# Prompt attention in plain fp32, two heads at a time, in place of products of high and low parts

## The chip, the cores and the metric

One core of one Trainium2 chip runs the whole program in one launch. The metric is the time of one execution in device microseconds (us); lower is better. The core's engines are called PE (matrix products), PEld (the loading of the stationary operand into PE), DVE (vector), ACT (scalar functions and copies), POOL (the second vector engine) and SP (which issues most DMAs). PE's array has 128 rows, over which a product sums, and 128 columns, its output partitions.

## The reference

One layer of a hybrid decoder for a prompt of 1024 tokens and for 8 x 8 sampled tokens. The input projection is split among an RWKV-7 recurrence, a short convolution and stick-breaking attention; then come an output projection, a squared-ReLU MLP and a gated per-layer embedding. What matters here is the attention of the prompt, 8 heads of 64 dimensions over 1024 positions:

```python
z = jnp.einsum('bqhd,bkhd->bhqk', q_blk.astype(jnp.float32), kf) * scale + bias_f
mask = k_pos[None, :] < q_pos[:, None]
log_beta = jnp.where(mask, jax.nn.log_sigmoid(z), -jnp.inf)
log_keep = jnp.where(mask, jax.nn.log_sigmoid(-z), 0.0)
later = lax.cumsum(log_keep, axis=3, reverse=True) - log_keep
wts = jnp.exp(log_beta + later)
return jnp.einsum('bhqk,bkhd->bqhd', wts, vf)
```

with `q` and `k` normalised per head beforehand (`rmsnorm`). In the recurrence, the keys are normalised per head too (`kk * lax.rsqrt(jnp.sum(kk * kk) + 1e-12)`).

## The kernel before

Large products run on PE in a reduced fp32 format (F32R, "fp32r" in the profile), which PE multiplies faster and less exactly than plain fp32 (F32). To keep fp32's accuracy an operand is split into a high part (a copy rounded to F32R, on ACT) and a low part (the remainder, by a subtraction on DVE or POOL), and a product is the sum of products of the parts. Small products, of the recurrence above all (lines 541 to 671, and 740 to 785 for the sampled tokens), are in plain fp32 and use halves or quarters of the array: an operand on partitions 0 to 63 or 64 to 127 sits in one row half, an output on such partitions in one column half.

The prompt's attention takes four steps.
- `project` (L847) writes the rows of q, k, v of 128 tokens. For v it makes a tile `spl` with a head's 64 high columns next to its 64 low ones and stores it in the DRAM scratch `v_s`. `stack` (L870) transposes q and k and stores high and low parts in the scratch `stk_s`, so that a head has 128 rows: 64 high, 64 low.
- `prep` (L932) loads, for one head, `stk_k`, `stk_q`, the swapped `stk_x` (low over high) and `vs`.
- `weights` (L952) makes, for one head and a block of 256 queries (two tiles of 128), the scores in chunks of up to 512 keys: L961 multiplies keys with `stk_q`, L962 adds the product with `stk_x`, so that all four products of parts are in. ACT takes two sigmoids of each chunk (L963, L964), POOL masks the diagonal (L968), DVE scans (L970) and multiplies (L972; on POOL for every other tile in the second call). The result is `beta`.
- `values` (L975) transposes `beta` (L990), splits it into `wth` and `wtl` (`split`, L59: ACT copies, DVE subtracts, L60 and L61), and multiplies both with `vs` (L1000, L1001), which gives the sums with v's high and low columns in the two halves of the output's partitions; L1003 and L1004 add them.

`attention` runs twice: for queries 0 to 511 it is interleaved by `run` with the convolution (`CA` says how many steps of each), for queries 512 to 1023 it follows the output projection of the first 512 tokens. `AA` and `AB_` say how many units `weights` runs ahead of `values`. Scores have two PSUM banks (`zbank`), transposed weights two (`wbank`), outputs one (`obank`).

The order in which the instructions stand on each engine is set when the program is built: a scheduler with a model of the times goes through what is ready, so attention's instructions end up woven into those of the convolution (L173 to L175), the output projection and the MLP's first products (L1144 to L1146), and not in the order in which they are written. Each engine then runs its row in that order.

Of the kernel before, what the change touches and what calls it, by code (L numbers as in the profile page):

```python
# [42 lines left out]
AA = 2  # L43
CA = (5, 4)
AB_ = 2
# [3 lines left out]
def hybrid_step(ctx: ExitStack, tc: tile.TileContext, I, O):  # L49
# [6 lines left out]
    def f(t):  # L56
        return t.bitcast(F32)

    def split(dst_hi, dst_lo, src):  # L59
        S.copy(dst_hi, src)  # L60
        V.tensor_sub(dst_lo, src, f(dst_hi))  # L61
# [29 lines left out]
    stk_s = dram.tile([2, 8, 2, 64, NP], F32, name="stk_s")  # L91
    v_s = dram.tile([8, 8, 128, 128], F32, name="v_s")
# [29 lines left out]
    ident_r = consts.tile([128, 128], F32R)  # L122
    G.tensor_copy(ident_r, ident)
# [276 lines left out]
    for j in range(2):  # L400
# [13 lines left out]
        rbs = []  # L414
        for a in range(2):
            rb = pe_tile("rb", F32R)
            rbs.append((rb, rp.tile([128, 2, 64], F32R, name=f"rb8{a}")))
            for d, i0, i1 in ((rb[:, :1024], 0, 8), (rbs[a][1].rearrange("p s d -> p (s d)"), 8, 9)):
                d = d.rearrange("p (i s d) -> p i s d", i=i1 - i0, s=2)
                src = rk[:, i0:i1, :, None].to_broadcast([128, i1 - i0, 2, 64])  # L420
                if a == 0:
                    V.tensor_copy(d, src)
                else:
                    h = rbs[0][0][:, :1024] if i0 == 0 else rbs[0][1].rearrange("p s d -> p (s d)")
                    V.tensor_sub(d, src, f(h).rearrange("p (i s d) -> p i s d", i=i1 - i0, s=2))
        for t0, n in CH:
            ps = tr()
            for t in range(t0, t0 + n, 128):
                r = min(128, T - t)
                for a in range(2):  # L430
# [395 lines left out]
    def sample_rows(n, w):  # L826

        both = sbp.tile([128, 8, 128], F32R, name="both", tag="nat", bufs=3)
# [9 lines left out]
        out, low = (sbp.tile([128, 512], F32, name=f"nats{e}", tag="st", bufs=4)[:64] for e in range(2))  # L838
# [10 lines left out]
    def project(n, ps, i0, nat, i):  # L849
# [11 lines left out]
        if n == 2:  # L861
            src = flat.rearrange("p (h d) -> p h d", h=8)
            for hf in range(2):
                hs = slice(4 * hf, 4 * hf + 4)
                spl = sbp.tile([128, 4, 128], F32R, name="spl", tag="st", bufs=4)
                S.copy(spl[:, :, 0:64], src[:, hs])
                G.tensor_sub(spl[:, :, 64:128], src[:, hs], f(spl[:, :, 0:64]))
                SP.dma_start(v_s[hs, i0 + i].rearrange("h p e -> p h e"), f(spl))

    def stack(hf, n, i0, nat):  # L870
# [9 lines left out]
        hl = [sbp.tile([128, 2, 256], F32R, name=f"st{e}", tag="st", bufs=4) for e in "hl"]  # L880
# [10 lines left out]
    for n in (2, 0, 1):  # L891
# [6 lines left out]
        for i0 in range(0, 8, 2):  # L898
            if i0 == 6:
                sample_rows(n, w)  # L900
            nat = sbp.tile([128, 2, 512], F32, name="nat", tag="nat", bufs=3)
# [21 lines left out]
    def attention(ap, q0, q1, zbank, wbank, obank, AHEAD):  # L923
# [6 lines left out]
        heads = {}  # L930

        def prep(h):  # L932

            stk = []
            for name, n, r0 in (("k", 1, 0), ("q", 0, 256 * q0), ("x", 0, 256 * q0)):
                r = slice(r0, 256 * q1)
                o = ap.tile([128, 256 * q1 - r0], F32R, name=f"stk_{name}", bufs=2)
                if name == "x":
                    for e in range(2):
                        SP.dma_start(f(o)[64 * e:64 * e + 64], stk_s[n, h, 1 - e, :, r])  # L940
                else:
                    SP.dma_start(f(o), stk_s[n, h, :, :, r].rearrange("e d t -> (e d) t"))
                stk.append(o)
            vs = ap.tile([128, 2 * q1, 128], F32R, name="vs", bufs=2)
            SP.dma_start(f(vs), v_s[h, 0:2 * q1].rearrange("i p e -> p i e"))
            heads[h] = stk + [vs]

        wts = {}

        def weights(h, qb):  # L950
            kk, qa, qx, _ = heads[h]
            for i in (2 * qb, 2 * qb + 1):  # L952
                L = 128 * (i + 1)
                q = slice(i * 128 - 256 * q0, i * 128 + 128 - 256 * q0)
                beta = ap.tile([128, 256 * q1], F32, name="beta", bufs=2 * AHEAD + 2)
                keep = ap.tile([128, 256 * q1 + 1], F32, name="keep", bufs=3 if q0 else 2)
                G.memset(keep[:, L:L + 1], 1.0)
                for c0 in range(0, L, 512):
                    n = min(512, L - c0)
                    pz = zbank()  # L960
                    PE.matmul(pz[:, :n], qa[:, q], kk[:, c0:c0 + n], start=True, stop=False)  # L961
                    PE.matmul(pz[:, :n], qx[:, q], kk[:, c0:c0 + n], start=False, stop=True)  # L962
                    S.activation(beta[:, c0:c0 + n], pz[:, :n], AF.Sigmoid, bias=bias[:, 0, h:h + 1])  # L963
                    S.activation(keep[:, c0:c0 + n], pz[:, :n], AF.Sigmoid, bias=bias[:, 1, h:h + 1], scale=-1.0)  # L964

                for t, fill in ((keep, 1.0), (beta, 0.0)):
                    own = t[:, L - 128:L]
                    G.affine_select(own, own, pattern=[[-1, 128]], compare_op=ALU.is_ge, fill=fill, base=-1,  # L968
                                    channel_multiplier=1)
                V.tensor_tensor_scan(keep[:, 0:L][:, ::-1], keep[:, 0:L][:, ::-1], onesq[:, 0:1].to_broadcast([128, L]),  # L970
                                     1.0, op0=ALU.mult, op1=ALU.mult)
                (G if i % 2 and q0 else V).tensor_mul(beta[:, 0:L], beta[:, 0:L], keep[:, 1:L + 1])  # L972
                wts[h, i] = beta

        def values(h, qb):  # L975
            vs = heads[h][3]
            pr, s = divmod(h, 2)
            d = slice(64 * s, 64 * s + 64)
            po = obank()
            last_kt = 2 * qb + 1  # L980
            for g in range(qb + 1):
                pw = wbank()
                wh = ap.tile([128, 2, 256], F32R, name="wth", bufs=2)
# [25 lines left out]
        for n in range(len(units) + AHEAD):  # L1009
            if n < len(units):  # L1010
                if n % (q1 - q0) == 0 and units[n][0] < 7:
                    prep(units[n][0] + 1)
                weights(*units[n])
# [674 lines left out]
```

## Time and profile before

| | us |
|---|---|
| median of 3 runs | 1679.89 (1678.74 to 1680.69) |
| the profiled execution | 1685.16 |
| its span | 1683.5 |
| PE busy | 1627.7 |
| DVE busy | 1052.4 |
| ACT busy | 791.9 |
| POOL busy | 716.8 |

The page's parts are: busy time of each engine; the span in slices; DMA queues; the chain of work that ended last; the costliest groups of instructions; DMA issues. Beside the page, the trace answers for any stretch: busy time by stretch, waits (who waited, for whom, how long), and the timeline (start, length, engine, line, what is written from what, shape of the array part as rows*columns, shape of the moving operand). A matmul's record contains the time in which its result runs out of the array, in which the next may already have started: what it costs the engine is the distance between its start and the next start.

### The profile page before, as it was taken

To read this page: it belongs to the slowest core of one execution; us is meant where nothing else is said; L and a number is where in the kernel's file an instruction comes from. 1 tells how busy PE (TensorE), PEld (TensorE's weight loads), DVE (VectorE), ACT (ScalarE), POOL (GpSimd) and SP (SyncE) were. 2 spreads that over 40 slices of the span, in tenths; PEclk is the share of its full clock that TensorE was granted. 3 is DMA by queue.
4 is the path that set the end of the run, shared out by engine and by line. 5 is a ranking of instruction groups with operands and counts; after the bars stand their busy time and mean duration, and the time that the engine had idled before them with its cause. 6 is when DMAs were issued, how large, how long until landed. Compare 5 with 4: busy or idle time off the path is not lost.

```text
span 1683.5 us, 29402 instructions
## 1 busy us (share of the span) xinstructions
PE 1627.7 (97%) x11229; PEld 1435.7 (85%) x11229; DVE 1052.4 (63%) x1822; ACT 791.9 (47%) x1583; POOL 716.8 (43%) x799
## 2 busy tenths in 40 slices
PE   5999999999998999999999999999999999999998
PEld 5999777778897777888887778988999999999898
DVE  5366834455389679878754345277777776768432
ACT  6733235334256467666543444374444444437321
POOL 5221412133255454433435644367555545638210
PEclk8999999999999999999999999999999999999999
DMA  6134575444445453443245556322222232322211
GB/s 206 65 119 138 159 184 135 108 111 120 115 130 175 146 156 105 129 128 106 80 140 167 175 160 213 92 76 89 87 90 89 86 92 88 98 76 88 72 46 41
DMA packets 201470, 196.93 MB, mean 117 GB/s; under 512 B 57969, under 2 KB 161425, under 8 KB 201202
## 3 DMA queue, kind: packets, MB, share of 16 engines
q1 hardware_dynamic: 189330, 173.52, 34.6%
q0 software_dynamic: 5120, 16.78, 3.2%
q10 hardware_dynamic: 6880, 4.75, 1.2%
q8 instruction: 88, 1.44, 0.4%
q14 instruction: 52, 0.43, 0.1%
HBM read 158.03 MB, written 36.98 MB: 116 GB/s over the span
## 4 chain that ended last, share of the span: by engine, by line
PE 49%; DVE 4%; DMA 3%; ACT 1%; issue 1%; POOL 1%; ACTq 0%; DVEq 0%; POOLq 0%; SPq 0%
PE b L1144 11%; PE b L1145 11%; PE b L1146 11%; PE b L1501 3%; PE b L1502 3%; PE b L1503 3%; DMA wr<-in_w_up 1%; PE b L990 1%; PE b L1269 1%; DMA wr<-in_w_down 1%; PE b L1001 1%; PE b L1000 1%; DMA kpg<-in_cache_k,idx 1%; DVE x L1541 1%; PE b L1250 1%
## 5 line engine op out<-in xcount | busy, mean ns | idle before, releaser
L1125 POOL TENSOR_TENSOR wl<-wr,wh 128x512 fp32r<-128x512 f32 x137 | 198.0, 1450 | 207.7 <-ACT wh L1124 190.8
L1541 DVE TENSOR_TENSOR x<-b,x 128x288 f32<-128x288 f32 (+1 forms) x384 | 198.3, 528 | 86.7 <-PE b L1146 85.6
L1124 ACT CAST wh<-wr 128x512 fp32r<-128x512 f32 x233 | 143.8, 622 | 220.6 <-PE b L1145 153.4
L1144 PE MATMUL b<-ah,wh 128*128 128x288 f32 (+1 forms) x612 | 202.2, 331 | 2.5 <-DVE x L1541 1.4
L1146 PE MATMUL b<-ah,wl 128*128 128x288 f32 (+1 forms) x612 | 200.7, 328 | 0.0
L1145 PE MATMUL b<-al,wh 128*128 128x288 f32 (+1 forms) x612 | 200.7, 328 | 0.0
L1144 PE MATMUL b<-nh,wh 128*128 128x512 f32 (+1 forms) x352 | 131.5, 374 | 5.7 <-DVE x L1456 2.1
L1145 PE MATMUL b<-nl,wh 128*128 128x512 f32 (+1 forms) x352 | 130.4, 370 | 0.0
L1146 PE MATMUL b<-nh,wl 128*128 128x512 f32 (+1 forms) x352 | 130.0, 370 | 0.0
L1144 PEld LDWEIGHTS b<-ah,wh 128*128 128x128 f32 x612 | 114.8, 188 | 13.1 <-DVE x L1541 3.9
L1145 PEld LDWEIGHTS b<-al,wh 128*128 128x128 f32 x612 | 115.0, 188 | 8.2 <-issue 0.8
L1146 PEld LDWEIGHTS b<-ah,wl 128*128 128x128 f32 x612 | 114.9, 188 | 8.0
L173 PE MATMUL b<-h_hi,wh 128*128 128x384 f32 (+1 forms) x336 | 114.7, 341 | 1.3 <-ACT xs L353 0.6
L174 PE MATMUL b<-h_lo,wh 128*128 128x384 f32 (+1 forms) x336 | 113.8, 339 | 0.0
L175 PE MATMUL b<-h_hi,wl 128*128 128x384 f32 (+1 forms) x336 | 112.3, 334 | 0.0
L970 DVE TENSOR_TENSOR_SCAN keep<-keep,onesq 128x128 f32<-128x128 f32 (+3 forms) x64 | 98.5, 1539 | 16.7 <-POOL keep L968 16.1
L161 POOL TENSOR_TENSOR wl<-wr,wh 128x512 fp32r<-128x512 f32 x40 | 54.9, 1387 | 103.4 <-ACT wh L158 102.5
L1125 POOL TENSOR_TENSOR wsl<-s,wsh 128x512 fp32r<-128x512 f32 x60 | 79.0, 1337 | 35.9 <-ACT wsh L1124 29.0
L1125 DVE TENSOR_TENSOR wl<-wr,wh 128x512 fp32r<-128x512 f32 x96 | 75.5, 789 | 25.3 <-ACT wh L1124 21.8
L1144 PEld LDWEIGHTS b<-nh,wh 128*128 128x128 f32 x352 | 66.4, 189 | 17.4 <-DVE x L1456 2.5
L908 PE MATMUL b<-wl,h_hi 128*128 128x512 f32 x192 | 77.7, 405 | 1.8 <-DVE wl L161 1.8
L908 PE MATMUL b<-wh,h_hi 128*128 128x512 f32 x192 | 78.5, 411 | 0.0
(471 smaller groups left out, 4655.2 us busy)
## 6 DMA issues: line engine op xcount, KB each, us to landing
wr<-in_w_up SPq DMA_DIRECT2D x64, 512.0 KB
wr<-in_w_down SPq DMA_DIRECT2D x64, 512.0 KB
wr<-in_w_in SPq DMA_DIRECT2D x26, 512.0 KB
wr<-in_w_out SPq DMA_DIRECT2D x16, 512.0 KB
xt<-in_x_prompt SPq DMA_DIRECT2D x8, 512.0 KB
v_s<-spl SPq DMA_DIRECT2D x16, 256.0 KB
stk_s<-sth ACTq DMA_DIRECT2D x32, 128.0 KB
stk_s<-stl SPq DMA_DIRECT2D x32, 128.0 KB
```

The source lines that it names most:

```text
L161: sub[k0 // step % 2].tensor_sub(lo, raw[:, c:c + 512], f(hi))
L173: PE.matmul(ps[:, :n], wh[k][:, c], a, start=(k == 0), stop=False)
L174: PE.matmul(ps[:, :n], wh[k][:, c], b, start=False, stop=False)
L175: PE.matmul(ps[:, :n], wl[k][:, c], a, start=False, stop=(k == nk - 1))
L908: last = PE.matmul(ps[i], x[:, t0:t0 + 128], wt, start=start, stop=stop)
L970: V.tensor_tensor_scan(keep[:, 0:L][:, ::-1], keep[:, 0:L][:, ::-1], onesq[:, 0:1].to_broadcast([128, L]), 1.0, op0=ALU.mult, op1=ALU.mult)
L1124: S.copy(h3, src)
L1125: (sub or G).tensor_sub(l3, src, f(h3))
L1144: PE.matmul(ps[:, :n], w(0, k, m), a, start=(k == 0), stop=False)
L1145: PE.matmul(ps[:, :n], w(0, k, m), b, start=False, stop=False)
L1146: PE.matmul(ps[:, :n], w(1, k, m), a, start=False, stop=(k == nk - 1))
L1541: V.tensor_add(p.x[:, m, t0:t0 + n], ps[:, :n], p.x[:, m, t0:t0 + n])
```

## The change

Two heads that share a tile of 128 partitions (a pair) are worked on together, in plain fp32.
- `project` and `stack` store v, q and k unsplit (scratch `v_s` and `qk_s`), with one DMA per two tiles, and no `spl`, `sth`, `stl` are made. `prep` loads three tiles per pair, once for two heads.
- `weights` takes a pair: each product of scores is one fp32 matmul per head, with 64 rows, head 0 in the upper row half and head 1 in the lower, into the two score banks.
- `values` takes a pair: the transposed weights are copied once (ACT) and not split; one fp32 matmul per head and key tile, with 64 columns, head 0 in the one column half and head 1 in the other, into one output bank. One ACT copy of 128 partitions takes the result out.
- `AA`, `AB_` become 1 (in pairs), `CA` becomes (5, 2); tiles get other buffer numbers (`nat` 4, `keep` 3, `beta` by its length).
- In the recurrence's key normalisation, the spread of the reciprocal norms is one fp32 transpose per 128 tokens in place of two F32R matmuls with an identity (L431), and `rb` is no longer split.

```diff
-AA = 2
-CA = (5, 4)
-AB_ = 2
+AA = 1
+CA = (5, 2)
+AB_ = 1
...
-            for t in range(t0, t0 + n, 128):
-                r = min(128, T - t)
-                for a in range(2):
-                    PE.matmul(ps[:, t - t0:t - t0 + r], rbs[a][0][:, t:t + 128] if t < NP else rbs[a][1].rearrange("p s d -> p (s d)"),
-                              ident_r[:, 128 - r:], start=a == 0, stop=a == 1)
+            for t in range(t0, min(t0 + n, NP), 128):
+                PE.transpose(ps[:, t - t0:t - t0 + 128], rb[:, t:t + 128], ident)
+            if t0 + n == T:
+                PE.transpose(ps[:, n - 128:n], rb8.rearrange("p s d -> p (s d)"), ident)
...
-        if n == 2:
-            src = flat.rearrange("p (h d) -> p h d", h=8)
-            for hf in range(2):
-                hs = slice(4 * hf, 4 * hf + 4)
-                spl = sbp.tile([128, 4, 128], F32R, name="spl", tag="st", bufs=4)
-                S.copy(spl[:, :, 0:64], src[:, hs])
-                G.tensor_sub(spl[:, :, 64:128], src[:, hs], f(spl[:, :, 0:64]))
-                SP.dma_start(v_s[hs, i0 + i].rearrange("h p e -> p h e"), f(spl))
+            SP.dma_start(v_s[i0:i0 + 2].rearrange("i p c -> p i c"), nat)
...
-        S.copy(hl[0], raw)
-        V.tensor_sub(hl[1], raw, f(hl[0]))
-        for e in range(2):
-            for s in range(2):
-                (S, SP)[e].dma_start(stk_s[n, 4 * hf + s:4 * hf + 4:2, e, :, i0 * 128:i0 * 128 + 256]
-                                     .rearrange("r d t -> d r t"),
-                                     f(hl[e])[64 * s:64 * s + 64])
+        SP.dma_start(qk_s[n, 2 * hf:2 * hf + 2, :, i0 * 128:i0 * 128 + 256].rearrange("r p t -> p r t"), raw)
...
-                    pz = zbank()
-                    PE.matmul(pz[:, :n], qa[:, q], kk[:, c0:c0 + n], start=True, stop=False)
-                    PE.matmul(pz[:, :n], qx[:, q], kk[:, c0:c0 + n], start=False, stop=True)
+                    pz = [zbank() for _ in range(2)]
+                    for s in range(2):
+                        PE.matmul(pz[s][:, :n], q[hs(s), qs], k[hs(s), c0:c0 + n], start=True, stop=True)
...
-                if g < qb:
-                    split(wh, wl, p3)
-                else:
-                    split(wh[:, 0], wl[:, 0], p3[:, 0])
-                    split(wh[:, 1, 128:], wl[:, 1, 128:], p3[:, 1, 128:])
+                    if g < qb:
+                        S.copy(w, p3)
+                    else:
+                        S.copy(w[:, 0], p3[:, 0])
+                        S.copy(w[:, 1, 128:], p3[:, 1, 128:])
...
-                    PE.matmul(po[:, c], vs[:, kt, :], wh[:, e, c], start=kt == 0, stop=False)
-                    PE.matmul(po[:, c], vs[:, kt, :], wl[:, e, c], start=False, stop=kt == last_kt)
+                    for s in range(2):
+                        PE.matmul(po[hs(s), c], vs[:, kt, hs(s)], wt[s][:, e, c], start=kt == 0, stop=kt == last_kt)
             o32 = ap.tile([128, 256], F32, name="o32", bufs=2)
-            S.copy(o32[d], po[64 - 64 * s:128 - 64 * s, 0:256])
-            V.tensor_add(o32[d], po[d, 0:256], o32[d])
-            SP.dma_start(mix_s[4 + pr, d, qb * 256:qb * 256 + 256], o32[d])
+            S.copy(o32, po[:, 0:256])
+            SP.dma_start(mix_s[4 + pr, :, qb * 256:qb * 256 + 256], o32)
```

Where the instructions stand in the built programs: on PE in the first call of attention, before, values and then scores of one head (b is a PSUM bank; the last number is output partitions x columns; x4 is four alike).

```order
L1000 MATMUL b_5343<-wth,vs 128x256
L1001 MATMUL b_5343<-wtl,vs 128x256
L1000 MATMUL b_5343<-wth,vs 128x256
L1001 MATMUL b_5343<-wtl,vs 128x256
L1000 MATMUL b_5343<-wth,vs 128x256
L1001 MATMUL b_5343<-wtl,vs 128x256
L1000 MATMUL b_5343<-wth,vs 128x128
L1001 MATMUL b_5343<-wtl,vs 128x128
L961 MATMUL b_5434<-stk_k,stk_q 128x384
L962 MATMUL b_5434<-stk_k,stk_x 128x384
L961 MATMUL b_5448<-stk_k,stk_q 128x512
L962 MATMUL b_5448<-stk_k,stk_x 128x512
```

All of these use the full array, and they follow each other. On PE of the changed program in the same call, the scores of a pair over 512 keys (now L933; L963 is the transpose, L168 and L169 are the convolution's products):

```order
L933 MATMUL b_5137<-kT,qT 128x512
L963 MATMUL b_5158<-ident,beta_5013 128x128
L963 MATMUL b_5158<-ident,beta_5039 128x128 x2
L963 MATMUL b_5165<-ident,beta_5014 128x128
L963 MATMUL b_5165<-ident,beta_5040 128x128 x2
L168 MATMUL b_5314<-h_lo_85,wh 128x320
L933 MATMUL b_5138<-kT,qT 128x512
L169 MATMUL b_5314<-h_hi_83,wl 128x320
```

The two heads' matmuls, written one after the other, have six transposes and one product of the convolution between them. On PE of the changed program, a little later, values of a pair (now L976, 64 output partitions):

```order
L976 MATMUL b_5648<-wt_5654,vs 64x256
L963 MATMUL b_5667<-ident,beta_5439 128x128
L963 MATMUL b_5667<-ident,beta_5465 128x128 x2
L976 MATMUL b_5648<-wt_5661,vs 64x256
L976 MATMUL b_5648<-wt_5654,vs 64x256
L976 MATMUL b_5648<-wt_5661,vs 64x256
```

The first head's first matmul (`wt_5654`) has three transposes between it and the second head's (`wt_5661`); the other three follow each other.

More of the change, by code (lines that the diff above doesn't have):

```diff
@@ L121, in hybrid_step @@
     make_identity(nc, ident)
-    ident_r = consts.tile([128, 128], F32R)
-    G.tensor_copy(ident_r, ident)
     bones = consts.tile([128, 128], F32)
@@ L826, in sample_rows @@
     def sample_rows(n, w):
-        both = sbp.tile([128, 8, 128], F32R, name="both", tag="nat", bufs=3)
+        both = sbp.tile([128, 8, 128], F32R, name="both", tag="nat", bufs=4)
         for e in range(2):
@@ L837, in sample_rows @@
                       stop=(m, k) == (128, 7))
-        out, low = (sbp.tile([128, 512], F32, name=f"nats{e}", tag="st", bufs=4)[:64] for e in range(2))
+        out, low = (sbp.tile([128, 512], F32, name=f"nats{e}", bufs=1)[:64] for e in range(2))
         S.copy(low, ps[64:128])
@@ L928, in attention @@
         V.tensor_scalar(bias[:, 1], bias[:, 0], -1.0, None, op0=ALU.mult)
[L930 to L946, printed above, removed]
@@ L948, in attention, with prep @@
-        wts = {}
-        def weights(h, qb):
-            kk, qa, qx, _ = heads[h]
+        pairs = {}
+        span = 256 * (q1 - q0)
+        def prep(pr):
+            k = ap.tile([128, 256 * q1], F32, name="kT", bufs=2)
+            q = ap.tile([128, span], F32, name="qT", bufs=2)
+            vs = ap.tile([128, 2 * q1, 128], F32, name="vs", bufs=2)
+            SP.dma_start(k, qk_s[1, pr, :, 0:256 * q1])
+            SP.dma_start(q, qk_s[0, pr, :, 256 * q0:256 * q1])
+            SP.dma_start(vs, v_s[0:2 * q1, :, 128 * pr:128 * pr + 128].rearrange("i p c -> p i c"))
+            pairs[pr] = k, q, vs
@@ L952, in weights, with hs @@
+        def hs(s):
+            return slice(64 * s, 64 * s + 64)
+        def weights(pr, qb):
+            k, q, _ = pairs[pr]
+            wts = {}
             for i in (2 * qb, 2 * qb + 1):
                 L = 128 * (i + 1)
[L954 to L957, printed above, removed]
+                qs = slice(i * 128 - 256 * q0, i * 128 + 128 - 256 * q0)
+                beta = [ap.tile([128, 256 * q1 - 128 + 128 * (i % 2)], F32, name=f"beta{i % 2}", bufs=2 * AHEAD + 2)
+                        for _ in range(2)]
+                keep = [ap.tile([128, 256 * q1 + 1], F32, name="keep", bufs=3) for _ in range(2)]
+                for s in range(2):
+                    G.memset(keep[s][:, L:L + 1], 1.0)
@@ L958, in weights @@
                 for c0 in range(0, L, 512):
                     n = min(512, L - c0)
-                    pz = zbank()
[L961 to L978, printed above, removed]
+                    pz = [zbank() for _ in range(2)]
+                    for s in range(2):
+                        PE.matmul(pz[s][:, :n], q[hs(s), qs], k[hs(s), c0:c0 + n], start=True, stop=True)
+                    for s in range(2):
+                        h = 2 * pr + s
+                        S.activation(beta[s][:, c0:c0 + n], pz[s][:, :n], AF.Sigmoid, bias=bias[:, 0, h:h + 1])
+                        S.activation(keep[s][:, c0:c0 + n], pz[s][:, :n], AF.Sigmoid, bias=bias[:, 1, h:h + 1],
+                                     scale=-1.0)
@@ new lines, in weights @@
+                for s in range(2):
+                    for t, fill in ((keep[s], 1.0), (beta[s], 0.0)):
+                        own = t[:, L - 128:L]
+                        G.affine_select(own, own, pattern=[[-1, 128]], compare_op=ALU.is_ge, fill=fill, base=-1,
+                                        channel_multiplier=1)
+                    V.tensor_tensor_scan(keep[s][:, 0:L][:, ::-1], keep[s][:, 0:L][:, ::-1],
+                                         onesq[:, 0:1].to_broadcast([128, L]), 1.0, op0=ALU.mult, op1=ALU.mult)
+                    (G if i % 2 and q0 else V).tensor_mul(beta[s][:, 0:L], beta[s][:, 0:L], keep[s][:, 1:L + 1])
+                    wts[s, i] = beta[s]
@@ L979, in values @@
+            return wts
+        def values(pr, qb, wts):
+            vs = pairs[pr][2]
             po = obank()
```

58 lines of the change are left out of this document (25 added, 33 removed).

## The prediction

> **What bounds the kernel now.** I read the page's first part, then the busy time by stretch of the span from the projections to the last attention unit, then PE's waits there, then PE's timeline row by row, since a busy share hides what one matmul costs the next.
>
> ```profile
> span 1683.5 us, 29402 instructions
> PE 1627.7 (97%) x11229; PEld 1435.7 (85%) x11229; DVE 1052.4 (63%) x1822; ACT 791.9 (47%) x1583; POOL 716.8 (43%) x799
> ```
>
> PE leaves 56 us of the span. By stretch (start:end, length, busy us of PE, PEld, DVE, ACT, POOL, then the granted clock):
>
> ```profile
> 350.00:450.00 100.00, 100.00 (x1000) 83.43 (x1001) 43.90 (x100) 35.47 (x75) 33.83 (x37) 1.00 0.38 102
> 450.00:500.00 50.00, 46.70 (x394) 43.32 (x391) 35.33 (x64) 25.80 (x58) 23.63 (x46) 0.97 0.45 136
> 500.00:550.00 50.00, 45.71 (x287) 37.27 (x287) 44.56 (x76) 35.22 (x79) 27.33 (x55) 0.90 0.59 180
> 550.00:600.00 50.00, 45.80 (x275) 36.30 (x274) 30.73 (x79) 21.18 (x46) 19.11 (x28) 0.93 0.58 168
> 600.00:650.00 50.00, 45.21 (x208) 36.49 (x207) 44.73 (x43) 37.48 (x70) 26.75 (x34) 0.97 0.36 106
> 650.00:700.00 50.00, 47.32 (x251) 39.42 (x250) 46.14 (x56) 31.82 (x64) 20.16 (x31) 1.00 0.40 119
> 800.00:870.00 70.00, 70.00 (x377) 60.14 (x376) 46.67 (x71) 36.61 (x72) 26.59 (x26) 1.00 0.30 88
> ```
>
> Attention lies between 457 and 866 us, woven into convolution, output projection and the first MLP matmuls. PE idles 3.3 + 4.3 + 4.2 + 4.8 + 2.7 = 19.3 us of 450 to 700, and the lowered clock takes (0.03 + 0.10 + 0.07 + 0.03) x 50 = 11.5 us of full-speed time more; after 800 PE is never idle. So what the change adds to PE lengthens the run, and at most 31 us can be won back from waits. Of these, attention's own helpers cause the smaller part (engine and line that waited, for whom, us, times, longest):
>
> ```profile
> PE b L1000 <- DVE o L1004: 5.5, 2, 4.0
> PE b L1000 <- ACT wth L60: 1.4, 1, 1.4
> PE b L990 <- DVE beta L972: 0.9, 1, 0.9
> ```
>
> **What PE pays today.** Scores, then values, in the timeline (start us, length us, line); the price of one is the distance to the next start:
>
> ```profile
> 709.77 0.39 PE L962 MATMUL b<-stk_k,stk_x 128*128 128x512 f32 x1
> 710.00 0.22 PE L961 MATMUL b<-stk_k,stk_q 128*128 128x128 f32 x1
> 710.07 0.27 PE L962 MATMUL b<-stk_k,stk_x 128*128 128x128 f32 x1
> 710.18 0.45 PE L1145 MATMUL b<-nl,wh 128*128 128x512 f32 x1
> ...
> 835.00 0.28 PE L1000 MATMUL b<-wth,vs 128*128 128x256 f32 x1
> 835.11 0.28 PE L1001 MATMUL b<-wtl,vs 128*128 128x256 f32 x1
> ...
> 835.95 0.49 PE L990 MATMUL b<-ident,beta 128*128 128x128 f32 x3
> ```
>
> 512 columns cost 0.23, 128 cost 0.09 in the mean of 0.07 and 0.11, and 256 cost (835.95 - 835.00) / 8 = 0.119, eight standing there without a gap; I put 384 at 0.175, between its neighbours. By the loops there are 48, 16, 16 and 16 score products of 512, 384, 256 and 128 columns, two matmuls each: 2 x (11.0 + 2.8 + 1.9 + 1.4) = 34.4 us. Values: 256 x 0.119 + 64 x 0.09 = 36.2 us. Together 70.6 us.
>
> **What a plain fp32 matmul in half the array costs.** The recurrence already does it. L541 is fp32 in row halves (64 of 128 rows), L765 in column halves; each fp32 matmul leaves two records.
>
> ```profile
> 463.31 0.34 PE L173 MATMUL b<-h_hi,wh 128*128 128x384 f32 x1
> 463.58 0.71 PE L541 MATMUL b<-ar,bk 64*128 64x128 f32 x4
> 464.22 0.45 PE L174 MATMUL b<-h_lo,wh 128*128 128x384 f32 x1
> 464.50 0.34 PE L175 MATMUL b<-h_hi,wl 128*128 128x384 f32 x1
> ...
> 220.40 0.71 PE L541 MATMUL b<-ar,bk 64*128 64x128 f32 x8
> 221.04 0.50 PE L908 MATMUL b<-wl,h_hi 128*128 128x512 f32 x1
> ...
> 387.75 1.16 PE L541 MATMUL b<-ar,bk 64*128 64x128 f32 x8
> 388.84 0.27 PE L665 MATMUL b<-Rm,St 64*64 64x64 f32 x2
> ...
> 511.77 0.39 PE L990 MATMUL b<-ident,beta 128*128 128x128 f32 x2
> 512.09 1.08 PE L765 MATMUL b<-um,AB 128*64 128x512 f32 x4
> 513.10 0.44 PE L990 MATMUL b<-ident,beta 128*128 128x128 f32 x2
> ...
> 543.23 1.07 PE L765 MATMUL b<-um,AB 128*64 128x512 f32 x2
> 544.24 0.33 PE L1000 MATMUL b<-wth,vs 128*128 128x128 f32 x1
> ```
>
> Three things are to be seen. First, halves overlap only when they stand next to each other: at 220.40 four matmuls, two in each half, take 0.64 us, as long as two in one half at 463.58; the pair at 512.09 takes 1.01, the lone one at 543.23 also 1.01. At 387.75 the scheduler had put four of one half by themselves: 1.09, nothing shared. Second, a visit to the half array costs by itself: 1.09 - 0.64 = 0.45 for two more matmuls means 0.225 each, so a lone one of 128 columns is 0.64 - 0.225 = 0.415, of which 0.19 is the visit. Third, its neighbours pay: the full-array matmul ahead of 463.58 took 0.27 where 384 columns cost 0.175 (+0.095), the first behind it 0.28 (+0.105).
>
> **The change on PE.** The order shown with the change above gives the counts. Scores of two heads were written side by side, yet in the place shown the two halves stand seven full-array matmuls apart; in the place with the values, four matmuls that could be two rounds make three rounds in two visits, a transpose run between them. Over the whole order, 39 of the 48 score pairs are split; the 96 score matmuls make 87 rounds (45, 16, 14, 12 of 512, 384, 256, 128 columns), each a visit. The 160 value matmuls make 116 rounds (99 of 256, 17 of 128 columns) in 78 visits.
>
> **The sum.** A lone round costs 0.415 at 128 columns (L541) and 1.01 at 512 (L765); on the line between, 0.61 at 256 and 0.81 at 384.
> - Scores: 12 x 0.415 + 14 x 0.61 + 16 x 0.81 + 45 x 1.01 = 72.0 us.
> - Values: 99 x 0.61 + 17 x 0.415, less 0.19 for the 38 rounds that share a visit: 60.2 us.
> - Edges: 127 visits start from the full array (12.1 us at 0.095); 50 end on a matmul of the other kind (0.105) and 83 on a transpose or its like, where I take 0.055, between nothing and 0.105: 9.8 us.
> - Before: -70.6. Transposes in attention stay 288.
> - Key normalisation: 36 matmuls become 18 transposes, at about 0.11 each (the two at 511.77 take 0.32 with an edge of 0.1): -2.
>
> That is +81 us of PE work. No row shows 64 rows with 512 columns: its passes alone (1.01 - 0.19 = 0.82) and the slope of L541 (0.19 + 4 x 0.225 = 1.09) bound it, -8 to +4 us over 45 rounds; I take the L765 value, nearest in columns.
>
> What goes elsewhere: DVE loses the low parts
>
> ```profile
> L61 DVE TENSOR_TENSOR wtl<-b,wth 128x512 fp32r<-128x512 f32 x48 | 32.3, 679 | 9.4 <-ACT wth L60 9.2
> L963 ACT ACTIVATE beta<-b,bias 128x512 f32<-128x512 f32 x48 | 33.2, 691 | 13.9 <-PE b L962 10.1 <-PE b L990 3.1
> ```
>
> (their smaller shapes too) and the addition at L1004; ACT copies as often as it cast. The splits of q, k and v, their SP, ACT and POOL work and half of the scratch traffic lie mostly under a PE that is busy 100 of 100 us (350 to 450): nothing, and if that cover were gone it could only help. The attention waits above, 5.5 + 1.4 + 0.9 = 7.8 us, lose their cause or meet a later PE; with some of the clock back I take -13, between 0 and -31. The sum: +68 us, a span of about 1751. The profiled execution took 1685.16 us, 5 over the median 1679.89, so the median goes to 1679.9 + 68 = 1748.
>
> **Rivals.** *The halves meet anyway* (ends faster). If PE drew the late half up to the early one, there would be 48 score rounds (39.0 us) and 80 value rounds in 40 visits (64 x 0.61 + 16 x 0.415 - 40 x 0.19 = 38.1), edges 88 x 0.18 = 15.8: 92.9 - 70.6 - 2 = +20, and with all 31 us of waits gone, 1669. It decides faster only where more than 20 us of waits go. For it, PE does let a later line start before an earlier one has finished, in free quarters of the array (eight matmuls of L565 stand ahead of eight of L577):
>
> ```profile
> 277.35 0.51 PE L565 MATMUL b<-UV,AB 64*64 64x64 f32 x10
> 277.64 0.27 PE L577 MATMUL b<-TT,LM 64*64 64x64 f32 x2
> 277.69 0.28 PE L565 MATMUL b<-UV,AB 64*64 64x64 f32 x3
> ```
>
> Against it, full-array matmuls stand between, and 387.75 shows a half left alone. The Trainium skill, "TensorE: Matmul & The Clock Gate", section "The mechanism", says that matmuls start and end strictly in program order; by that rule this rival is out and 1748 stands, though the rows at 277.64 differ from it within the tiled array. The Trainium skill, "TensorEngine Tiling (Array Packing)", sections "Theoretical Speedup" and "Key Properties", gives up to twice the speed for 64 rows or columns with tiles running independently; taken for every pair that is this rival's 1669 to 1700, and the lone L765 at 543.23 speaks against it.
>
> *New waits on the score banks* (slower still). A pair fills both score banks, so the next scores wait for four sigmoids, 4 x 0.69 = 2.8 us; behind that matmul PE's whole queue stands, projection included. If each of 48 products exposes 0.7 us: +34, 1782. Against it, other work stands between most pairs, and ACT is busy under 38 of 50 us.
>
> *The extra work falls into idle time.* All 31 us return and the rounds cost their lower bound: 81 - 8 - 31 = +42, 1722.
>
> **Numbers.** Forecast 0.78, bank waits 0.10, idle time 0.07, halves meet 0.05. The range runs from 1716, a little under the idle-time case, to 1786, just past the bank waits. Changes under 0.2% (3.4 us) count as none: slower 0.94, same 0.02, faster 0.04, the last two from the case of meeting halves.
>
> **What would show it.** Right: in the changed profile a lone L933 of 512 columns is followed by its successor after about 1.0 us, 160-odd visits with a longer matmul on either side, PE idle under 10 us between 450 and 900, and all of the loss between the first score and the last unit. Wrong: halves starting some ns apart though the order splits them, or PE waiting on sigmoids.

## The result, and the profile after

The changed kernel takes 1725.21 us (median of 4 runs, 1723.51 to 1727.19) where the kernel before, beside it, takes 1680.06: a ratio of 1.027, with a 95% interval of 1.0252 to 1.0288. It is 45 us slower, where 68 had been forecast. On a second chip it stood at 1733.66 to 1691.06, 1.0253 (1.0236 to 1.0271). Chips differ by some 0.6%, so the runs below are compared by their ratios, and a difference of ratios is turned into us on 1680. A difference from the changed kernel is given as a range, since that kernel has two ratios, 1.0253 and 1.027.

The head of the page, first its span, then each engine's busy time:

```profile
span 1721.5 us, 28842 instructions
PE 1685.5 (98%) x11211; PEld 1397.7 (81%) x11211; DVE 968.8 (56%) x1658; ACT 772.4 (45%) x1535; POOL 697.5 (41%) x782
```

PE's busy time rose by 57.8 us, the span only by 38.0: PE's idle time fell from 55.8 to 36.0 us. By stretch, with the columns as before; first the kernel before in a stretch that the prediction did not show, then the kernel after:

```profile
200.00:250.00 50.00, 45.63 (x284) 34.94 (x282) 21.99 (x45) 19.43 (x39) 11.29 (x16) 0.93 0.69 172
```

```profile
200.00:250.00 50.00, 50.00 (x362) 39.31 (x360) 17.88 (x37) 16.66 (x34) 4.75 (x8) 1.00 0.54 140
...
450.00:500.00 50.00, 50.00 (x352) 36.44 (x351) 34.07 (x52) 28.59 (x70) 22.27 (x57) 1.00 0.20 68
500.00:550.00 50.00, 50.00 (x279) 29.58 (x277) 35.13 (x49) 31.83 (x71) 26.05 (x45) 1.00 0.42 134
550.00:600.00 50.00, 45.96 (x253) 30.92 (x252) 25.36 (x60) 22.11 (x45) 22.43 (x32) 0.97 0.49 151
600.00:650.00 50.00, 50.00 (x202) 28.27 (x203) 40.33 (x32) 36.64 (x68) 28.12 (x32) 1.00 0.23 72
650.00:700.00 50.00, 50.00 (x209) 28.18 (x207) 29.28 (x28) 28.53 (x59) 17.10 (x30) 1.00 0.23 74
```

Of the 19.3 us in which PE was idle between 450 and 700, 4.0 are left, and of the 11.5 us of lowered clock 1.5. The stretch at 200 to 250 had 4.4 us of idle PE and a clock of 0.93, and has neither now; the prediction had not looked there. PE's waits from 200 to 950 us (engine and line that waited, for whom, us, times, longest), the first rows:

```profile
PE b L1328 <- DVE x L1331: 2.3, 2, 1.9
PE b L880 <- ACT sq L790: 1.8, 1, 1.8
PE b L1119 <- ACT x L1429: 1.2, 1, 1.2
```

None of these is a wait of attention: the 7.8 us for `o`, `wth` and `beta` are gone, and no score waits for a sigmoid.

What a half-array matmul costs, in PE's timeline (start, length, line, out and in, array part, moving operand; two records make one plain fp32 matmul):

```profile
641.17 0.40 PE L1120 MATMUL b<-nl,wh 128*128 128x512 f32 x1
641.49 1.12 PE L933 MATMUL b<-kT,qT 64*128 64x512 f32 x2
642.54 0.50 PE L1121 MATMUL b<-nh,wl 128*128 128x512 f32 x1
642.98 1.08 PE L976 MATMUL b<-wt,vs 128*64 128x256 f32 x6
643.98 0.33 PE L963 MATMUL b<-ident,beta 128*128 128x128 f32 x1
...
648.70 0.40 PE L1121 MATMUL b<-nh,wl 128*128 128x512 f32 x1
649.03 0.70 PE L933 MATMUL b<-kT,qT 64*128 64x256 f32 x2
649.65 0.50 PE L1119 MATMUL b<-nh,wh 128*128 128x512 f32 x1
```

A score matmul of 512 columns that stands alone takes 1.05 us, one of 256 columns 0.62. The full-array matmul ahead takes 0.32 where its like takes 0.23, the one behind 642.98 - 642.54 = 0.44, which is 0.23 with an edge on either side (0.11 and 0.10). With the distances from start to start added up over all rows, the scores cost 75.4 us (forecast 72.0) and the values 57.5 us (forecast 60.2); the rows show 140 visits (a score next to a value counts as one visit; the edges of the prediction were worked out for 133).

### The profile page after: what moved, and what is told of

It reads as the page before. It is cut to its first block, busy times and chain, and to the rows that moved or that the text cites. A ratio compares the mean times of both kernels' runs of the same rounds, so it can differ in the third digit from the quotient of the medians.

```text
span 1721.5 us, 28842 instructions
## 1 busy us (share of the span) xinstructions
PE 1685.5 (98%) x11211; PEld 1397.7 (81%) x11211; DVE 968.8 (56%) x1658; ACT 772.4 (45%) x1535; POOL 697.5 (41%) x782
## 4 chain that ended last, share of the span: by engine, by line
PE 88%; DMA 4%; DVE 3%; ACT 2%; POOL 1%; issue 1%; SPq 0%; ACTq 0%; DVEq 0%; POOLq 0%
PE b L1119 13%; PE b L1120 13%; PE b L1121 13%; PE b L880 8%; PE b L933 4%; PE b L167 3%; PE b L976 3%; PE b L168 3%; PE b L169 3%; PE b L1476 3%; PE b L1478 3%; PE b L1477 3%; PE b L963 3%; DMA wr<-in_w_up 1%; PE b L527 1%
## 5 line engine op out<-in xcount | busy, mean ns | idle before, releaser
L1100 POOL TENSOR_TENSOR wl<-wr,wh 128x512 fp32r<-128x512 f32 x137 | 190.4, 1393 | 276.9 <-ACT wh L1099 257.5
L945 DVE TENSOR_TENSOR_SCAN keep<-keep,onesq 128x128 f32<-128x128 f32 (+7 forms) x64 | 97.1, 1517 | 54.9 <-POOL keep L943 52.2
L168 PE MATMUL b<-h_lo,wh 128*128 128x384 f32 (+1 forms) x336 | 112.9, 336 | 0.0
L169 PE MATMUL b<-h_hi,wl 128*128 128x384 f32 (+1 forms) x336 | 112.2, 334 | 0.0
L1100 POOL TENSOR_TENSOR wsl<-s,wsh 128x512 fp32r<-128x512 f32 x60 | 78.6, 1329 | 37.5 <-ACT wsh L1099 30.7
L936 ACT ACTIVATE beta<-b,bias 128x512 f32<-128x512 f32 (+3 forms) x96 | 55.9, 582 | 68.0 <-PE b L933 62.6
L155 POOL TENSOR_TENSOR wl<-wr,wh 128x512 fp32r<-128x512 f32 x40 | 55.4, 1398 | 74.5 <-ACT wh L152 74.3
L933 PE MATMUL b<-kT,qT 64*128 64x512 f32 (+3 forms) x192 | 81.2, 536 | 0.0
```

What stands on the lines that cost most here:

```text
L168: PE.matmul(ps[:, :n], wh[k][:, c], b, start=False, stop=False)
L169: PE.matmul(ps[:, :n], wl[k][:, c], a, start=False, stop=(k == nk - 1))
L933: PE.matmul(pz[s][:, :n], q[hs(s), qs], k[hs(s), c0:c0 + n], start=True, stop=True)
L945: V.tensor_tensor_scan(keep[s][:, 0:L][:, ::-1], keep[s][:, 0:L][:, ::-1], onesq[:, 0:1].to_broadcast([128, L]), 1.0, op0=ALU.mult, op1=AL ...
L1100: (sub or G).tensor_sub(l3, src, f(h3))
```

## The experiments

**1. The halves side by side.** The later half of each pair, and the value products that follow the first, are put at the front of what is ready and kept in program order.

```diff
-                    for s in range(2):
-                        PE.matmul(pz[s][:, :n], q[hs(s), qs], k[hs(s), c0:c0 + n], start=True, stop=True)
+                    for s in (1, 0):
+                        with tc.high_priority() if s == 0 else ExitStack():
+                            mm = PE.matmul(pz[s][:, :n], q[hs(s), qs], k[hs(s), c0:c0 + n], start=True, stop=True)
+                        if s == 0:
+                            tc.keep_in_program_order(mm)
```

> The changed kernel with the second head's matmul written first and the first head's pinned right behind it, so that 36 of 48 score pairs and most value pairs stand side by side in PE's order (96 + 160 matmuls make 60 + 100 rounds in 121 visits, before 87 + 116 in 165). Theory (a split pair is paid twice, a visit 0.19 us and its edges): by the same prices the attention products and edges fall from 154 to 119 us, so the time falls by about 35 us, to about 1690. Rival (the halves overlap anyway, the loss lies elsewhere): within 5 us of 1725.

Measured: 1.0125 (1.0108 to 1.0142), 22 to 24 us faster than the changed kernel. In the timeline:

```profile
641.90 0.48 PE L1127 MATMUL b<-al,vh 128*128 128x512 f32 x1
642.31 0.49 PE L934 MATMUL b<-kT,qT 64*128 64x128 f32 x4
642.73 0.50 PE L1128 MATMUL b<-ah,vl 128*128 128x512 f32 x1
...
656.39 0.70 PE L934 MATMUL b<-kT,qT 64*128 64x256 f32 x4
657.02 0.50 PE L1126 MATMUL b<-ah,wh 128*128 128x512 f32 x1
```

At 656.39 two matmuls of 256 columns take 0.63 us; at 649.03 above, one by itself took 0.62. Adjacent, the second half is free; apart, it costs the whole price again. The Trainium skill, "TensorEngine Tiling (Array Packing)", section "Theoretical Speedup", gives the two halves up to twice the speed; these rows agree where the halves are neighbours in PE's row, and only there. By the rows the scores fell to 53.7 and the values to 49.0 us, 30 us less, and 111 visits in place of 140 spare some edges too; 22 to 24 us came through. The rest went into waits that came back. Busy time from 450 to 900, after and then with the halves side by side:

```profile
450.00:900.00 450.00, 445.96 (x2330) 283.77 (x2329) 258.78 (x327) 245.15 (x498) 193.36 (x291) 1.00 0.31 95
```

```profile
450.00:900.00 450.00, 434.42 (x2333) 291.90 (x2332) 273.26 (x343) 245.32 (x501) 206.31 (x286) 0.99 0.31 94
```

PE's idle time there rises from 4.0 to 15.6 us once PE is earlier.

**2. No half array in the second call's scores.** These are made in plain fp32 over all 128 rows, with the other head's rows of q set to zero.

```diff
-                        PE.matmul(pz[s][:, :n], q[hs(s), qs], k[hs(s), c0:c0 + n], start=True, stop=True)
+                        if q0:
+                            PE.matmul(pz[s][:, :n], padded[pr, qb][s][:, 128 * (i % 2):128 * (i % 2) + 128],
+                                      k[:, c0:c0 + n], start=True, stop=True)
```

> The changed kernel with the scores of the second call of attention (64 of 96 matmuls) in plain fp32 over the full array: q's other 64 rows are zeros, so the passes are those of a lone half and no visit is made. Theory (a visit costs 0.19 us and its edges 0.15 to 0.2): 64 matmuls cost about 46 us instead of 55 and 10 us of edges, less 2 us for three pairs that overlapped: 15 to 19 us faster, 1707 to 1711. Rival (what counts is the passes alone, visits are hidden): within 4 us of 1725.

Measured: 1.0148 (1.0129 to 1.0166), 18 to 20 us faster than the changed kernel, as the theory said. The timeline, a score between two transposes:

```profile
644.49 1.02 PE L943 MATMUL b<-kT,qT 128*128 128x512 f32 x2
645.35 0.27 PE L976 MATMUL b<-ident,beta 128*128 128x128 f32 x1
```

0.86 us for 512 columns over the full array, 1.05 alone in half of it: the visit costs 0.19, the value that the prediction took from L541, and the neighbours' edges go as well. A half that stands alone loses to a full array half of which multiplies zeros.

**3. PE later, and nothing else.** Before, with each score product made three times: 2 x 34.4 = 69 us more of full-array work.

```diff
+                    for _ in range(2):
+                        PE.matmul(pz[:, :n], qa[:, q], kk[:, c0:c0 + n], start=True, stop=False)
+                        PE.matmul(pz[:, :n], qx[:, q], kk[:, c0:c0 + n], start=False, stop=True)
                     PE.matmul(pz[:, :n], qa[:, q], kk[:, c0:c0 + n], start=True, stop=False)
```

> The kernel before with each score product made three times (the last one counts), full array, no visits: +69 us of PE work in the same stretch, all helpers as they were. Theory A (a PE that is later removes the waits and the lowered clock by itself): about 30 of the 69 us are absorbed, 1715 to 1725. Theory B (helpers leaving removed them): nearly all 69 us are seen, 1743 to 1749.

Measured: 1.0296 (1.0279 to 1.0314), +50 us. So 19 of 69 us are absorbed: between the two expectations, 11 short of the first. With 450 to 900 in the kernel before and then here:

```profile
450.00:900.00 450.00, 430.74 (x2533) 361.12 (x2530) 347.11 (x514) 267.23 (x542) 200.46 (x297) 0.97 0.44 131
```

```profile
450.00:900.00 450.00, 438.46 (x2679) 373.77 (x2678) 309.76 (x474) 248.23 (x505) 178.70 (x283) 0.98 0.41 119
```

11.5 of the 19.3 us of idle time stay, so waits that a later PE does not meet are 7.8 us of the 19; the clock there rose by 0.01, and the rest is not placed. From 200 to 250 nothing is won (44.3 us busy, clock 0.93): that stretch lies ahead of attention.

**4. DVE's helper back in the changed kernel.** An operation on DVE behind each copy of transposed weights, as long as the subtraction that the change removed.

```diff
+                    for to, fr in ((w, p3),) if g < qb else ((w[:, 0], p3[:, 0]), (w[:, 1, 128:], p3[:, 1, 128:])):
                         S.copy(to, fr)
+                        V.tensor_tensor(to, fr, to, op=ALU.max)
```

> The changed kernel with a DVE operation of the old subtraction's shapes put back behind each copy of the transposed weights (a maximum of the bank and its own copy, written in place: the values stay as they are), so DVE's work of about 55 us and its place in the chain to PE are back. The order is made anew: by counts its PE work is 9 us above the changed kernel's (91 value visits for 78). Theory A (waits went because PE became the later one): about +9, 1734. Theory B (waits went because DVE's part left): another 15 to 25 us on top, 1749 to 1759.

Measured: 1.032 (1.0301 to 1.0338), 8 to 11 us more than the changed kernel, as the first theory said. That theory expected 9 us from PE's work alone, since PE's order came out with more visits. The values did rise from 57.5 to 60.0 us by the rows, and PE's idle time between 450 and 900 from 4.0 to 8.9 us. So DVE's helper, put back, cost some 5 us at most by that idle time, and not the further 15 to 25 us of the second theory; how much of the 8 to 11 is its own is not shown.

**5. DVE's helper away in the kernel before.** `split` becomes a copy, and L1001 multiplies `wth` once more.

```diff
-                    split(wh, wl, p3)
+                    S.copy(wh, p3)
...
-                    PE.matmul(po[:, c], vs[:, kt, :], wl[:, e, c], start=False, stop=kt == last_kt)
+                    PE.matmul(po[:, c], vs[:, kt, :], wh[:, e, c], start=False, stop=kt == last_kt)
```

> Before without the low part of the transposed weights: the 64 subtractions on DVE (L61) are left out and the second of the two value products uses the high part once more, so PE does the same matmuls; the values come out doubled. Theory (DVE's helper work is a cause of its own of PE's waits between 450 and 900): with some 40 us less on DVE there, PE's idle time of 19.3 us falls by 5 to 12 and part of the 11.5 us of lowered clock returns: 8 to 16 us faster, ratio 0.990 to 0.995. Rival (the waits go only where PE comes later, as with the scores made three times): within 3 us of before, 0.998 to 1.002.

Measured: 0.9989 (0.9974 to 1.0005). The theory falls: taking 46 us from DVE between 450 and 900 bought 2 us, 4 at most, and PE's longest wait there became one for a DMA (`xr`, 7.7 us in two waits). PE's idle time there did not fall, it rose from 19.3 to 23.8 us. DVE was not the only one late; what it gives up, the next in line takes.

**6. The key normalisation alone**, unsplit as in the change, in the kernel before.

> Before with one edit of the change alone, the key normalisation unsplit: 18 fp32 transposes in place of 36 F32R matmuls, and no DVE subtraction for the low part of the spread norms. Theory (the waits and the lowered clock between 200 and 250 us hang on this edit): the two waits there, 2.5 and 1.8 us, go, the clock of that stretch rises from 0.93 to 1.00 (3.5 us), and with 2 us of PE work the time falls by 5 to 10 us, ratio 0.994 to 0.997. Rival (they hang on the other edits, or on nothing that the change does on purpose): at most the 2 us of PE work, ratio 0.998 to 1.000, and the stretch keeps 45.6 us of busy PE and clock 0.93.

Measured: 0.9967 (0.9954 to 0.998), 5.5 us faster than before. The time lies in the theory's band, its reason is refuted: the stretch keeps its idle time and its clock, and one wait for `bk` is longer than the two of before together.

```profile
200.00:250.00 50.00, 44.49 (x307) 34.74 (x306) 18.91 (x38) 17.06 (x35) 7.72 (x10) 0.93 0.68 167
```

```profile
PE b L533 <- DMA bk<-bk_s: 5.5, 1, 5.5
```

2 us are PE's 18 instructions less, by the prediction's price; where the other 3 or so come from stays open. Why the one wait is longer is seen in run 10.

**7. All of it without half arrays**: the scores three times, no low part of the transposed weights, the norms unsplit; +67 us on PE.

> Before with its scores made three times (+69 us of PE on the full array), without the low part of the transposed weights (values doubled) and with the key normalisation unsplit (-2 us): what the change adds to PE and frees beside it, without any half array. If these three account for the relief of the change (some 36 us), the time is 67 - 36 = 31 us over before, ratio 1.016 to 1.021. If the relief also needs the splits of q, k and v to be gone, or the half arrays' place in PE's order, it lies nearer the 1.030 that three-fold scores gave by themselves: 1.024 to 1.030.

With the changed kernel itself beside it on the same chip:

> The changed kernel as it is, beside the next three, so that their ratios can be set against its own on one chip. Expected 1.027 of before, as in the first comparison.

Measured: 1.0248 (1.0229 to 1.0266) against 1.0253: 67 us give +42, so 25 are absorbed. That is in the second band. PE waits 6.4 us for `bk` and is busy 43.65 of 50 us from 200 to 250, so what the change won there comes from none of these three edits.

**8. The traffic back.** The changed kernel with every store of q, k and v made a second time, to scratch that nothing reads.

```diff
+            SP.dma_start(v_x[i0:i0 + 2].rearrange("i p c -> p i c"), nat)
...
+        for r in range(2):
+            (S, SP)[r].dma_start(qk_x[n, 2 * hf + r, :, i0 * 128:i0 * 128 + 256], raw[:, r])
```

> The changed kernel with each store of q, k and v rows made once more into scratch that nothing reads, k and q in two DMAs, one of them on ACT's queue: the scratch traffic and the DMA issues that the change took away come back, and no arithmetic. Theory (the loads of bk come late between 200 and 250 us because SP's queue and the DMA engines hold the stores of parts): PE waits there again for bk, its busy time falls from 50.0 to about 45 us and the clock to 0.93, and the time rises by 5 to 9 us over the changed kernel, ratio to before 1.029 to 1.033 where that stands at 1.025 to 1.027. Rival (the traffic is free, the arithmetic of the splits counts): within 3 us of the changed kernel, 1.024 to 1.028.

Measured: 1.0233 (1.0212 to 1.0255); PE stays busy 50.0 at clock 1.00 from 200 to 250. The theory falls: 6.3 MB of stores and 36 more issues cost nothing that can be measured. The loads that the change took away were not put back.

**9. The arithmetic of the splits back**, with the tile buffers of before and no DMA.

```diff
+                    spl = sbp.tile([128, 2, 256], F32R, name="spl", tag="st", bufs=4)
+                    c = nat[:, i, 256 * hf:256 * hf + 256]
+                    S.copy(spl[:, 0], c)
+                    G.tensor_sub(spl[:, 1], c, f(spl[:, 0]))
...
+        hl = [sbp.tile([128, 2, 256], F32R, name=f"st{e}", tag="st", bufs=4) for e in "hl"]
+        S.copy(hl[0], raw)
+        V.tensor_sub(hl[1], raw, f(hl[0]))
```

> The changed kernel with the arithmetic of the splits of q, k and v put back (ACT copies, subtractions on DVE and POOL into tiles that nothing reads, tile buffers as before: nat 3, st 4), and no further DMA. Theory (SP's queue and traffic make the loads late): within 3 us of the changed kernel, ratio 1.024 to 1.028, PE at 200 to 250 us busy 50 and at clock 1.00. Rival (DVE and POOL hold what the recurrence needs there): PE's busy time there falls to about 45 us, the clock to 0.93, and the ratio rises to 1.029 to 1.033.

Measured: 1.0317 (1.0285 to 1.0349), 8 to 11 us more than the changed kernel. What the rival expected came, and the stretch is back as it was with the norms unsplit (44.49 us busy, a wait of 5.5 us): busy time, PE's wait, and then the two waits of SP's queue ahead of it.

```profile
200.00:250.00 50.00, 44.23 (x307) 34.84 (x307) 18.96 (x39) 16.84 (x34) 7.49 (x10) 0.93 0.55 140
```

```profile
PE b L527 <- DMA bk<-bk_s: 5.8, 1, 5.8
```

```profile
SPq L290 <- DVE base_X L289: 7.8, 1, 7.8
SPq L290 <- DVE base_X L288: 4.1, 1, 4.1
```

L290 stores `base_X`, the inverse of small triangles that DVE computes in a chain of products and sums. SP's queue stands at that store until DVE is done, and the loads of `bk` are behind it in the same queue. In the kernel before the same store (there L296) held the queue for 6.7 and 6.3 us; in the changed kernel for 0.4 us. The chain is slow for a reason that the timelines of DVE and POOL show together. Before, DVE, and POOL beside it:

```profile
171.17 0.38 DVE L294 TENSOR_TENSOR base_X<-base_X,base_Q 128x207 f32<-128x207 f32 x1
171.58 0.81 DVE L292 TENSOR_TENSOR base_Q<-base_Z,base_X 128x220 f32<-128x220 f32 x1
172.43 0.81 DVE L294 TENSOR_TENSOR base_X<-base_X,base_Q 128x220 f32<-128x220 f32 x1
...
174.97 0.41 DVE L292 TENSOR_TENSOR base_Q<-base_Z,base_X 128x240 f32<-128x240 f32 x1
175.42 0.83 DVE L294 TENSOR_TENSOR base_X<-base_X,base_Q 128x240 f32<-128x240 f32 x1
```

```profile
171.41 3.27 POOL L867 TENSOR_TENSOR spl<-nat,spl 128x256 fp32r<-128x256 f32 x4 [26.19 <-ACT spl L866]
175.12 1.72 POOL L867 TENSOR_TENSOR spl<-nat,spl 128x256 fp32r<-128x256 f32 x2 [0.44 <-ACT spl L866]
```

And the same sum in the changed kernel, with POOL idle beside it:

```profile
177.75 0.39 DVE L288 TENSOR_TENSOR base_X<-base_X,base_Q 128x220 f32<-128x220 f32 x1
```

While POOL subtracts, a DVE instruction of the same shape takes 0.81 us in place of 0.39; between POOL's two bursts, at 174.97, it is back at 0.41. This suggests a chain: v's split on POOL stretches work on DVE, that work holds a store, the store holds a queue, and PE waits for a load that has nothing to do with attention. The next run tests it link by link. The Trainium skill, "SBUF — State Buffer", section "SBUF: two separate sides", says that DVE with two operands in SBUF and POOL take the port pair in turns, the whole instruction long; the doubled durations agree.

**10. POOL's part alone**, in the changed kernel.

```diff
+            for c in range(0, 512, 128):
+                spl = sbp.tile([128, 128], F32, name="spl", bufs=1)
+                G.tensor_sub(spl, flat[:, c:c + 128], flat[:, 0:128])
```

> The changed kernel with nothing but POOL's part of v's split put back: 4 subtractions of 128x128 per tile of 128 tokens, on v's rows as soon as they are there, into a tile that nothing reads; no ACT copies, no DVE subtractions, no DMA, tile buffers as in the changed kernel. Theory (POOL's two-operand subtractions slow DVE's subtractions and products of two operands, so that the small triangular inverse ends later, the store of base_X in SP's queue waits for it and the loads of bk stand behind that store): DVE's base_X and base_Q work grows from 28.5 us to 33 to 37, SP waits over 5 us for base_X, PE waits for bk, busy 44 to 46 at clock 0.93 between 200 and 250 us, ratio 1.029 to 1.033. Rival (ACT's copies, DVE's own subtractions or the tile buffers did it when the whole split was put back): stretch at 50.0 and 1.00, ratio 1.024 to 1.028.

Measured: 1.0279 (1.0257 to 1.0301). DVE's part of the inverse, in groups (busy us and mean ns behind the count), in the changed kernel and then here:

```profile
L288 DVE TENSOR_TENSOR base_X<-base_X,base_Q 128x31 f32<-128x31 f32 (+23 forms) x46 | 14.9, 324 | 1.5
L286 DVE TENSOR_TENSOR base_Q<-base_Z,base_X 128x31 f32<-128x31 f32 (+23 forms) x46 | 13.6, 296 | 3.5 <-DMA base_Z<-l_s 2.1
```

```profile
L286 DVE TENSOR_TENSOR base_Q<-base_Z,base_X 128x31 f32<-128x31 f32 (+23 forms) x46 | 16.7, 364 | 3.6 <-DMA base_Z<-l_s 2.1
L288 DVE TENSOR_TENSOR base_X<-base_X,base_Q 128x31 f32<-128x31 f32 (+23 forms) x46 | 15.6, 339 | 1.5
```

28.5 us become 32.3 (36.9 with the whole split back, 37.5 before), and SP waits 5.0 us for `base_X`: the first two links are shown. The third did not follow: PE stays busy 49.7 at clock 1.00, and the time cannot be told from the changed kernel's. The second store of `base_X` leaves at 193.45 in the changed kernel, at 198.71 here and at 200.72 with the whole split back. But a store that is 2 us later does not make a wait of 5.8 us. PE's timeline shows what else differs; the first two products with `bk`, in the changed kernel and then with the whole split back:

```profile
205.73 0.49 PE L527 MATMUL b<-ar,bk 64*128 64x128 f32 x4
...
206.81 0.49 PE L527 MATMUL b<-ar,bk 64*128 64x128 f32 x4
```

```profile
205.85 0.80 PE L527 MATMUL b<-ar,bk 64*128 64x128 f32 x4 [5.77 <-DMA bk<-bk_s]
...
213.22 0.49 PE L527 MATMUL b<-ar,bk 64*128 64x128 f32 x4
```

The first starts at nearly the same time in both (206.77 in this run). What changed is PE's order: in the changed kernel and in this run 216 products of the projection, of 0.23 us each, stand ahead of it. With the whole split back only 196 do, and the other 20 follow behind it. Twenty such products are 4.6 of the 5.8 us, so the wait is for the most part one that the newly built order no longer covers, and some 1.2 us would be left for a later load. The same 196 stand ahead in the kernel before with the norms unsplit (run 6) and in run 7, which fits their longer waits. A late store can reach PE by itself, too: in the kernel before, 216 products stood ahead, the store left at 207.83, and PE waited 2.5 us. Which of ACT's copies, DVE's own subtractions and the buffers moved the order was not taken apart.

**11. Before, with the norms unsplit and v's low part on DVE.**

```diff
-                G.tensor_sub(spl[:, :, 64:128], src[:, hs], f(spl[:, :, 0:64]))
+                V.tensor_sub(spl[:, :, 64:128], src[:, hs], f(spl[:, :, 0:64]))
```

> Before with the key normalisation unsplit, as in the run that had this alone (0.9967), and v's low part subtracted on DVE in place of POOL: 16 instructions of about 0.4 us in DVE's own row. Theory (what counts is the time that DVE loses, to POOL or to its own instruction): DVE loses 16 x 0.4 = 6.4 us where POOL's took about as much from it, so nothing is won: 0.995 to 0.999 of before. Rival (DVE loses more to POOL than the instruction costs it itself): the inverse ends 4 us earlier or more, PE's wait for bk of 5.5 us shrinks, and the time falls to 0.990 to 0.994.

Measured: 1679.17 us to 1687.28, 0.9954 (0.9939 to 0.997): within the theory's band, not to be told from the 0.9967 with the norms alone, and 0.46% faster than before, the fastest of all here. Its profiled execution took twice as long as all the others, so its rows can't be read beside theirs, and whether the inverse ended earlier is not known.

## Why the prediction was right, and where its sum was off

- *PE bounds, and what is added lengthens the run*: right. PE is busy 98% of the span.
- *Halves overlap only as neighbours*: right, shown by the first experiment (0.63 us for two, 0.62 for one) and by the 22 to 24 us that it won back. The rival of meeting halves did not happen.
- *Prices of rounds, visits and edges*: right. Scores 75.4 for 72.0, values 57.5 for 60.2 (132.9 for 132.2); the visit 0.19; edges 0.09 in, 0.11 out, 0.055 at transposes, over all visits 13.3 + 10.2 = 23.5 us for 21.9. Of the bounds for 64 rows with 512 columns the upper one was nearer: 1.05 between 0.82 and 1.09, for 1.01.
- *+81 us of PE work*: right within what can be measured. With the measured prices the same sum is 132.9 + 23.5 - 70.6 - 2 = 84 us. Busy time gives less: +57.8 us, and up to 17 us less lost to the lowered clock (mean clock 0.986 over 1683.5 us before, 0.996 over 1721.5 after), so up to 75. What makes the difference of 9 stays open. A row can mislead here, as three transposes and a product in the kernel before show:

```profile
697.80 0.49 PE L990 MATMUL b<-ident,beta 128*128 128x128 f32 x3
698.05 0.48 PE L1144 MATMUL b<-ah,vh 128*128 128x512 f32 x1
698.36 0.40 PE L1145 MATMUL b<-al,vh 128*128 128x512 f32 x1
```

  The product seems to pay an edge, 0.31 us where 512 columns take 0.23. But the three transposes ahead of it take 0.25, where three cost 0.33 elsewhere. All four take 0.56, which is 3 x 0.11 + 0.23: the product only starts early, and there is no edge to be credited to the kernel before.
- *Relief of -13*: this is the term that was mis-sized. With 75 to 84 us of work the time rose by 45 us in the medians and by 38 in the two profiled executions, so at least 30 us came back. By the prediction's own way of counting, idle time and lowered clock, the two profiles show 37: PE's idle time fell by 19.8 us and the loss to the clock by 16.7. Of these, 25 lie between 450 and 700 us, where the prediction had allowed 31 at most and taken 13, and 8 between 200 and 250, where it had not looked. The runs reach about the same size. A later PE by itself absorbs 19 of 69 us; with DVE's helper and the split norms gone as well it is 25 of 67; and the arithmetic of the splits of q, k and v, put back, costs 8 to 11. These parts come from different kernels; that they add up to about the whole is a fit and not a proof.
- *The splits of q, k and v lie under a busy PE, nothing*: wrong. The prediction checked 350 to 450 us; v's split runs on POOL from 171 to 206 us, into a stretch in which PE waited. Without the splits' arithmetic that wait is gone, and it came again with the arithmetic put back; there a part of it was a late load, and the larger part PE's newly built order. The second clause of the step, that losing the cover could only help, was right in sign.
- *Half of the scratch traffic is hidden*: right for the stores (+6.3 MB, no loss); the loads were not tried.
- *New waits on score banks*: not seen. *The extra work falls into idle time*: that rival was nearest, at 1722 for 1725, and it came so near by luck. Its rounds at their lower bound did not come (1.05 us for 0.82), and only 25 of its 31 us of waits and clock went; 8 us that it does not name, from 200 to 250, made up for part of this. The forecast of 1748 was 23 us too high.
- *All of the loss between the first score and the last unit*: the clock times do not show it. From the first score to the last value product the kernel took 408 us before (457.9 to 865.8) and takes 395 now (444.3 to 839.2), and what follows grew by 65 us. Between the two, PE now has 1134 other products where it had 1429: some 300 of them stand behind attention now. The loss is there by the prices of the rows, and the win ahead of the first score was missed.

## What to carry to other kernels

Packing two small products into halves of the array pays only if they are neighbours in the order that PE really runs, so read the built order; a half by itself costs the whole round, a visit and two edges (in this kernel 0.19 us for the visit and up to 0.2 for the edges). Where a bound engine shares its span with waits, work added to it is partly absorbed (here 19 of 69 us by the delay alone), and work taken from it gives less than its price, since waits come back (22 to 24 of 30 or more). Before an edit is costed at nothing, look at where its first and last instructions run, follow each engine it touches to the queues behind, and compare the built orders: here copies and subtractions on other engines, put back with their tile buffers, moved 20 products of PE behind one that waits for a load.

## What was not expected of the hardware

- DVE's two-operand instructions take twice as long while POOL subtracts: 0.81 us for 0.39 at 128x220.
- Two matmuls in opposite row halves, 256 columns each, take 0.63 us, and one alone 0.62; alone in a half array, 512 columns of plain fp32 take 1.05 us, over the full array 0.86.
- The first F32R product behind a plain fp32 transpose takes 0.31 us from its start to the next, where its like takes 0.23, but it starts 0.08 us early: three transposes and the product take 0.56, the sum of their usual prices. Distances tell the price over a whole run of rows, not at one seam.
